# Sums of squares along rows on ScalarE, key stores on ScalarE's queue, and a new order of the preparation steps

## The chip, the cores and the metric

The kernel runs on one core of a Trainium2 chip. The metric is the device time of one execution in microseconds (us). A run of this kernel is timed several times; the runs shown agree within 2.4 us. A profile of one further execution gives the engines' timelines: TensorE (PE in the profile, its weight loads PEld), VectorE (DVE), ScalarE (ACT), GpSimd (POOL) and SyncE (SP), which here only issues DMAs. ScalarE can issue DMAs too, on a queue of its own.

## The reference

One layer over 2048 latent tokens and 256 context tokens of width 1024, all in float32. What matters here is how it begins: each token is normalized, scaled and shifted, and then projected by one wide matrix.

```python
def _rmsnorm(x, g):
    xf = x.astype(jnp.float32)
    xf = xf * lax.rsqrt(jnp.mean(xf * xf, axis=-1, keepdims=True) + EPS)
    return (xf * g.astype(jnp.float32)).astype(x.dtype)
...
        mod = jax.nn.silu(c) @ w_ada[i] + b_ada[i]
        mod_c = jax.nn.silu(c_ctx) @ w_ada[i] + b_ada[i]
        shift, scale, gate = mod[:, None, :D], mod[:, None, D:2 * D], mod[:, None, 2 * D:]
...
        h_lat = _rmsnorm(x, norm_g[i]) * (1.0 + scale) + shift
        h_ctx = _rmsnorm(ctx, norm_g[i]) * (1.0 + scale_c) + shift_c
...
    na_q, na_k, na_v, na_g, r_q, r_k, r_v, r_g = _split_proj(h_lat @ w_in)
    cna_q, cna_k, cna_v, cna_g, cr_q, cr_k, cr_v, cr_g = _split_proj(h_ctx @ w_in)
```

After the projection come a neighbourhood attention, a two-way retention, gates, an output projection, the residual and a last normalization. The change touches none of these.

## The kernel before

Tokens lie along the columns: h is kept as 8 slices of 128 features (k = 0 to 7) by tokens. The host hands the kernel x both as it is (rows of tokens) and transposed. A float32 product is made of three fast ones: each operand is split into a high part (hi) and the rest (lo), and TensorE adds hi by hi, hi by lo and lo by hi. So h has to be ready as hi and lo before TensorE can use it.

**Windows.** The first stage computes the attention keys, in five windows of tokens: windows 0 to 3 take 512 latent tokens each (block 0 to 3), window 4 the 256 context tokens. A window has 32 steps; one step is one feature slice k of one unit, which is three matmuls (`tform`, L357). The four units of a window are four groups of 128 key columns. In window 0 the steps of the four units are mixed in an order written out by hand (`STEPS`, L63), so that slices of h are used as they get ready; its units end at steps 24, 28, 30 and 31. In the other windows the units follow one another, 8 steps each.

**Preparation.** Between the steps the other engines prepare h. The order is written out by hand in `PLAN` (L39): each entry has the step after which it is issued, the action, and its numbers. Each engine works off its own instructions in the order in which they are issued, and so does each DMA queue; an instruction that waits holds up all that follow on its engine. Latent tokens are prepared in pieces of 256 (i = 0 to 7, i = 8 is the context), each in two halves of four slices (u = 0, 1). Piece i belongs to block i // 2. The actions for a piece, in order:

- `x` (`load_x`): load the transposed piece, two DMAs of 512 KB on SP's queue.
- `sq` (`squares`): ScalarE squares it, POOL and VectorE add the eight slices up to one.
- `cs` (`colsum`): TensorE adds over the 128 features of a slice by four tiny matmuls (L209).
- `rs` (`rstd`, `spread_copy`): VectorE scales the sum, POOL raises it to the power -1/2, VectorE copies this r into a tile `t0` of 128 columns per token group.
- `sp` (`spread`): TensorE turns it into a row of r for each token, in every partition (L227).
- `mu` (`spread_mul`): VectorE multiplies x by it (L241), one half at a time.
- `ab` (`prep_ab`): scale and shift, slice by slice, on VectorE (L272) or ScalarE (L274).
- `hl` (`prep_hl`): ScalarE casts to hi (L279), POOL or VectorE subtracts for lo (L283). Eight steps later SP stores the half for later use (`hS`, L253).

Block 0 (i = 0, 1) has `p` (`prep_first`, L255) in place of `ab` and `hl`, one slice at a time. The scale and shift come from the modulation, in four column groups u: `s` splits a weight, `m` multiplies (L311), `ar` (`ada_row`) copies the row out of PSUM, `af` (`ada_fin`) turns it into columns and finishes with `mods` (L332).

**Buffers.** The pool `st` has four tiles of 512 KB; weights of the first units, squares and the context piece go through it in turn. Tiles named `o` have two buffers; both the modulation rows and the evicted keys use them. PSUM has six banks for units, column sums and spreads.

**Evicting the keys** (`u_k`, L380). When a unit ends, ScalarE casts its PSUM bank into `o` (L383), VectorE subtracts for the rest (L384), and the tile is stored to `kS`, 512 KB in windows 0 to 3. `store` (L149) defers the DMA by a number of ticks; a tick comes at the end of each unit, after its eviction. With 1, the store is issued right behind the unit's own eviction. The queue for it is SP's until window 4, and ScalarE's from there on.

After window 4 follow the context units (L809), values, and the other projections.

Of the kernel before, what the change touches and what calls it, by code (L numbers as in the profile page):

```python
# [9 lines left out]
F32 = mybir.dt.float32  # L10
# [3 lines left out]
ALU = mybir.AluOpType  # L14
# [4 lines left out]
P = 128  # L19
# [63 lines left out]
def hybrid_kernel(ctx: ExitStack, tc: tile.TileContext, a: dict, out: bass.AP):  # L83
# [34 lines left out]
    def pool(st, name, bufs, **kw):  # L118
        return st.enter_context(tc.tile_pool(name=name, bufs=bufs, reuse_waits="tile", **kw))
# [11 lines left out]
    env = dict(pp=pool(psx, "pp", 6, space=PSUM), st=pool(sx, "st", 4, side="right"), queue=nc.sync)  # L131

    def ptile(p=None):
        return (p or env["pp"]).tile([P, 512], F32, name="mm")
# [58 lines left out]

    def squares(i):
        sqs[i] = []
        for u in range(2):
            sq = xsq[i][u] if i < 2 else env["st"].tile([P, KH, 256], F32, name="st")
            nc.scalar.activation(sq, raw[i][u], AF.Square)
            eng = (nc.gpsimd, nc.vector)[u]
            eng.tensor_tensor(sq[:, 0:2, :], sq[:, 0:2, :], sq[:, 2:4, :], ALU.add)  # L200
            eng.tensor_tensor(sq[:, 0, :], sq[:, 0, :], sq[:, 1, :], ALU.add)
            sqs[i].append(sq)
        nc.vector.tensor_tensor(sqs[i][0][:, 0, :], sqs[i][0][:, 0, :], sqs[i][1][:, 0, :], ALU.add)

    def colsum(*ii):
        pm = ptile(None if ii[0] < 4 else psm)
        for j, i in enumerate(ii):
            for t in range(2):
                nc.tensor.matmul(pm[:, 2 * j + t:2 * j + t + 1], sqs[i][0][:, 0, t * P:(t + 1) * P], one, start=True, stop=True)  # L209
            rms[i] = pm[:, 2 * j:2 * j + 2]  # L210

    def rstd(i):
        r = env["st"].tile([P, 2], F32, name="rs", bufs=4)
        nc.vector.tensor_scalar(r, rms[i], 1.0 / D, EPS, ALU.mult, ALU.add)
        nc.gpsimd.tensor_tensor(r, r, mhalf[:, 0:2], ALU.pow)
        rbs[i] = r

    def spread_copy(i):
        rbs[i, 1] = env["st"].tile([P, 2, P], F32, name="t0", bufs=2)
        nc.vector.tensor_copy(rbs[i, 1], rbs[i].unsqueeze(2).to_broadcast([P, 2, P]))  # L220
# [95 lines left out]
    def ada_row(u):  # L316
        rows[u] = op.tile([P, 2, 512], F32, name="o")[:, 0, :]
        n = 4 if SPL[u] else 2
        (nc.scalar.copy, nc.vector.tensor_copy)[u % 2](rows[u][0:n, :], aps[u][0:n, :])
# [60 lines left out]
    def u_k(w, c0, ct, b):  # L380
# [4 lines left out]
        store(kS[c0 % 512 // P + ct][:, :, tok], f(o)[:, :, :n])  # L385
# [81 lines left out]
    acts = dict(sq=squares, cs=lambda *i: colsum(*i), rs=lambda i: (rstd(i), spread_copy(i)), sp=lambda *i: spread(*i),  # L467
# [23 lines left out]
    def window(b):  # L491
        units = [u_k(w01, 512 + 256 * g, ct, b) for g in range(2) for ct in range(2)]
        left = [KC] * 4
        for n, u in enumerate(STEPS if b == 0 else [u for u in range(4) for _ in range(KC)]):
            if b == 4 and n == 0:
                env["queue"] = nc.scalar
# [1128 lines left out]
```

## Time and profile before

| | |
|---|---|
| median of 3 runs | 1353.99 us (1352.1 to 1354.42) |
| the profiled execution's own time | 1357.11 us |
| its span, first to last instruction | 1355.2 us |
| TensorE busy | 1310.4 us (97%) |
| VectorE, ScalarE, POOL busy | 834.4, 606.1, 578.2 us |
| window 0 begins, window 4 ends | about 27.5 and 163.9 us |

In the timeline a row has the start, the length, engine, line and operation, what it writes and reads, the shape, the count, and in brackets the idle time of the engine before it with what ended it. A wait for several things is put down to the one that came last in the profile. In the table by stretch, behind the stretch and its length, each engine has its busy time and, in brackets, its instructions, and then come the granted clock of TensorE as a share of full speed, the busy share of the DMA engines, and GB/s. Groups of instructions have the count, then busy time and the mean length in ns, then the idle time before them. DMA rows show the busy share of the DMA engines in tenths over 40 equal slices of the stretch.

### The profile page before, as it was taken

To read this page: it belongs to the slowest core of one execution; us is meant where nothing else is said; L and a number is where in the kernel's file an instruction comes from. 1 tells how busy PE (TensorE), PEld (TensorE's weight loads), DVE (VectorE), ACT (ScalarE), POOL (GpSimd) and SP (SyncE) were. 2 spreads that over 40 slices of the span, in tenths; PEclk is the share of its full clock that TensorE was granted. 3 is DMA by queue.
4 is the path that set the end of the run, shared out by engine and by line. 5 is a ranking of instruction groups with operands and counts; after the bars stand their busy time and mean duration, and the time that the engine had idled before them with its cause. 6 is when DMAs were issued, how large, how long until landed. Compare 5 with 4: busy or idle time off the path is not lost.

```text
span 1355.2 us, 23103 instructions
## 1 busy us (share of the span) xinstructions
PE 1310.4 (97%) x8236; PEld 1148.7 (85%) x8236; DVE 834.4 (62%) x1444; ACT 606.1 (45%) x1259; POOL 578.2 (43%) x569
## 2 busy tenths in 40 slices
PE   6999999999999999999999999999999899999997
PEld 2477999887898888998999889889999789888886
DVE  5686356776666754477767777776655634445345
ACT  4354343333633343555655466556642244333432
POOL 4442101545114664354535465655423154544442
PEclk9999999999999999999999999999999999999999
DMA  9386788565966657977587877776538888445433
GB/s 364 135 279 233 257 286 232 189 204 192 345 161 218 206 180 244 240 222 200 147 226 207 231 217 210 189 189 192 154 100 298 263 294 265 159 165 171 163 121 129
DMA packets 172086, 287.26 MB, mean 212 GB/s; under 512 B 17345, under 2 KB 92225, under 8 KB 170690
## 3 DMA queue, kind: packets, MB, share of 16 engines
q1 hardware_dynamic: 139554, 228.35, 56.1%
q10 hardware_dynamic: 32416, 57.42, 11.7%
q8 instruction: 66, 1.08, 0.3%
q14 instruction: 50, 0.41, 0.1%
HBM read 194.48 MB, written 91.23 MB: 211 GB/s over the span
## 4 chain that ended last, share of the span: by engine, by line
PE 77%; DVE 6%; DMA 6%; POOL 4%; issue 3%; ACT 3%; SPq 1%; ACTq 0%; POOLq 0%; DVEq 0%
PE mm L374 20%; PE mm L671 17%; PE mm L1466 11%; PE mm L363 7%; PE sS L1028 4%; PE tr L1055 3%; PE po L1076 3%; PE mm L1190 2%; PE mm L311 2%; PE tr L1057 2%; PE po L1078 2%; DMA v<-rvS 1%; POOL hlo L531 1%; PE mm L1378 1%; PE mm L1377 1%
## 5 line engine op out<-in xcount | busy, mean ns | idle before, releaser
L374 PE MATMUL mm<-whi,hlo 128*128 128x256 f32 x832 | 228.8, 283 | 1.4 <-DMA hlo<-cS 1.4
L374 PE MATMUL mm<-whi,hhi 128*128 128x256 f32 x768 | 224.5, 292 | 0.0
L374 PE MATMUL mm<-wlo,hhi 128*128 128x256 f32 x768 | 217.2, 283 | 0.0
L1059 ACT CAST pt<-tr 128x640 fp32r<-128x640 f32 (+1 forms) x128 | 95.6, 747 | 160.8 <-PE tr L1057 158.2
L1065 DVE TENSOR_TENSOR pt<-tr,pt 128x640 fp32r<-128x640 f32 (+1 forms) x128 | 113.9, 890 | 78.5 <-ACT pt L1059 77.1
L374 PEld LDWEIGHTS mm<-whi,hlo 128*128 128x128 f32 x832 | 156.7, 191 | 1.8 <-DMA hlo<-cS 1.7
L1048 POOL TENSOR_SCALAR sp<-sp,stt 128x640 f32<-128x640 f32 (+2 forms) x128 | 103.1, 808 | 106.8 <-DVE stt L1047 76.1
L374 PEld LDWEIGHTS mm<-whi,hhi 128*128 128x128 f32 x768 | 146.4, 191 | 0.0
L374 PEld LDWEIGHTS mm<-wlo,hhi 128*128 128x128 f32 x768 | 146.2, 190 | 0.2 <-DVE wlo L347 0.2
L625 POOL TENSOR_TENSOR whi<-st,whi 128x512 fp32r<-128x512 f32 x48 | 64.7, 1369 | 161.1 <-ACT whi L624 160.0
L1037 DVE CUSTOM_DVE_ANT_0 sp<-sS,nb 128x640 f32<-128x640 f32 (+2 forms) x128 | 105.6, 825 | 34.2 <-PE sS L1028 27.8
L1042 ACT ACTIVATE sp<-sp,stt 128x640 f32<-128x640 f32 (+2 forms) x128 | 107.4, 839 | 20.2 <-DVE stt L1037 19.1
L363 PE MATMUL mm<-hhi,whi 128*128 128x512 f32 x256 | 108.5, 424 | 0.0
L363 PE MATMUL mm<-hlo,whi 128*128 128x512 f32 x256 | 102.4, 400 | 6.0 <-DVE hlo L265 2.1
L1028 PE MATMUL sS<-k,q 128*128 128x256 f32 (+3 forms) x512 | 99.2, 316 | 5.4 <-DVE stt L1037 5.1
L363 PE MATMUL mm<-hhi,wlo 128*128 128x512 f32 x256 | 102.4, 400 | 0.3 <-DVE wlo L347 0.3
L1466 PE MATMUL mm<-wor,y 128*128 128x512 f32 x384 | 95.7, 398 | 2.1 <-DVE xt L1475 1.1
L671 PE MATMUL mm<-hhi,whi 128*128 128x512 f32 x336 | 97.4, 394 | 0.0
L1475 DVE TENSOR_TENSOR xt<-mm,xt 128x512 f32<-128x512 f32 x64 | 43.9, 687 | 83.9 <-PE mm L1466 83.9
L1028 PEld LDWEIGHTS sS<-k,q 128*128 128x128 f32 x512 | 82.8, 188 | 12.5 <-DVE stt L1037 8.7
L1466 PE MATMUL mm<-won,y 128*128 128x512 f32 x336 | 90.0, 406 | 0.0
L1466 PEld LDWEIGHTS mm<-wor,y 128*128 128x128 f32 x384 | 69.9, 188 | 18.5 <-issue 3.5
(258 smaller groups left out, 3039.6 us busy)
## 6 DMA issues: line engine op xcount, KB each, us to landing
st<-in_w_in_dram SPq DMA_DIRECT2D x64, 512.0 KB
q<-qS SPq DMA_DIRECT2D x64, 256.0 KB
hlo<-hS SPq DMA_DIRECT2D x20, 512.0 KB
k<-kS SPq DMA_DIRECT2D x16, 576.0 KB
kS<-o SPq DMA_DIRECT2D x16, 512.0 KB
vB<-o SPq DMA_DIRECT2D x64, 128.0 KB
qS<-o ACTq DMA_DIRECT2D x16, 512.0 KB
woS<-g ACTq DMA_DIRECT2D x32, 256.0 KB
```

The costliest lines, as they stand in the source:

```text
L363: nc.tensor.matmul(pm[:, :n], ww[:, k, cs], h[:, k, :], start=(k == 0 and i == 0), stop=(k == KC - 1 and i == 2))
L374: nc.tensor.matmul(pm[:, t * WG:(t + 1) * WG], h[:, k, o:o + P], ww[:, k, :], start=(k == 0 and i == 0), stop=(k == KC - 1 and i == 2))
L625: nc.gpsimd.tensor_tensor(t[:, 1], r, f(t)[:, 0], ALU.subtract)
L671: nc.tensor.matmul(pm, ww[:, k, :], hh[:, k, :], start=(k == 0 and i == 0), stop=(k == KH - 1 and i == 2))
L1028: nc.tensor.matmul(o, hd["q"][i][:, hl, j * P:(j + 1) * P], k, start=(hl == 0), stop=(hl == 1))
L1037: nc.vector.tensor_tensor_reduce(T["sp"][:, :n], T["s"], nbz[big][:, o:o + n], -1.0, 3e38, ALU.add, ALU.min, T["st"][:, 0:1])
L1042: nc.scalar.activation(sp[:, :n], sp[:, :n], AF.Exp, bias=st[:, 0:1], scale=-1.0, accum_out=st[:, 1:2])
L1048: nc.gpsimd.tensor_scalar(sp[:, :n], sp[:, :n], st[:, 2:3], 0.0, ALU.mult, ALU.add)
L1059: nc.scalar.copy(pt[:, :ng_ + 2, 0, :], tr[:, :ng_ + 2, :])
L1065: nc.vector.tensor_tensor(pt[:, :n, 1, :], tr[:, :n, :], f(pt)[:, :n, 0, :], ALU.subtract)
L1466: nc.tensor.matmul(pm, yy[:, k, :], ww[:, k, sl], start=(k == 0 and i == 0), stop=(k == 3 and i == 2))
L1475: nc.vector.tensor_tensor(xts[t][:, sl], pm, xts[t][:, sl], ALU.add)
```

## The change

- Pieces 2 to 8 get their sums of squares from x as rows of tokens. A new action `xt` loads two tiles of 128 tokens by 1024 features (512 KB each, on SP's queue, through `st`). `squares` is then two instructions of ScalarE, each of which also adds up along its row. The adds on POOL and VectorE and the four tiny matmuls of `cs` go for these pieces. Pieces 0 and 1 stay as they were.
- For pieces 2 to 8 the scaling of the sum and the copy into `t0` go from VectorE to POOL, where the power already is.
- The modulation row of group 2 is copied by VectorE, not ScalarE.
- Key stores are on ScalarE's queue from the start, and deferred by two ticks: the store of a unit is issued behind the next unit's eviction.
- `PLAN` is new: slices 7 and 6 of block 0 come at steps 17 and 18, ahead of the scaling of block 1; the `mu` of pieces 2 and 3 (first halves) moves to step 14; block 1's `hl` moves from steps 28 and 29 to 18 to 22; squares of pieces 5 and 6 both come at step 33, their `rs` at 35, spread 5 at step 40 (50 before); block 2's `hl` moves from steps 55 to 61 to 46 to 50. Loads of x and the new row loads are placed anew. From step 68 on the order is that of before, without `sq`, `cs` and `rs`.

```diff
-    (4, 's', 2, 0), (4, 'x', 4), (4, 'p', 2), (5, 'sq', 2), (7, 'm', 2, 0), (8, 'm', 2, 1), (9, 'p', 3),
...
+    (-1, 'p', 1), (-1, 'm', 1, 3), (-1, 'ws', 1), (0, 'ar', 1), (3, 'af', 1), (4, 'xt', 2), (4, 'xt', 3), (4, 'mu', 1, 1),
+    (4, 's', 2, 0), (4, 'x', 4), (4, 'p', 2), (7, 'm', 2, 0), (8, 'm', 2, 1), (9, 'p', 3), (9, 'sq', 2), (9, 'sq', 3),
+    (9, 'm', 2, 2), (9, 'm', 2, 3), (9, 'ar', 2), (10, 'xt', 4), (10, 'x', 5), (11, 'xt', 5), (12, 'mu', 0, 1),
+    (12, 'af', 2), (12, 'm', 3, 0), (12, 'p', 5), (12, 'm', 3, 1), (12, 'p', 4), (12, 'rs', 2), (12, 'rs', 3),
+    (13, 'm', 3, 2), (13, 'm', 3, 3), (13, 'ar', 3), (14, 'sp', 2, 3), (14, 'mu', 2, 0), (14, 'mu', 3, 0), (14, 'sq', 4),
+    (14, 'blk', 1), (15, 'xt', 6), (16, 'af', 3), (17, 'rs', 4), (17, 'p', 7), (18, 'p', 6), (18, 'x', 6),
+    (18, 'ab', 2, 0), (18, 'ab', 3, 0), (18, 'hl', 2, 0), (18, 'hl', 3, 0), (18, 'mu', 2, 1), (18, 'mu', 3, 1),
+    (19, 'ab', 2, 1), (20, 'ab', 3, 1), (21, 'hl', 2, 1), (22, 'hl', 3, 1), (26, 'sp', 4), (28, 'mu', 4, 0),
+    (30, 'mu', 4, 1), (33, 'sq', 5), (33, 'sq', 6), (35, 'rs', 5), (35, 'rs', 6), (36, 'xt', 7), (36, 'ab', 4, 0),
+    (38, 'x', 7), (40, 'sp', 5), (40, 'sq', 7), (41, 'mu', 5, 0), (42, 'rs', 7), (42, 'ab', 4, 1), (42, 'mu', 5, 1),
+    (43, 'ab', 5, 0), (45, 'blk', 2), (45, 'ab', 5, 1), (46, 'hl', 4, 1), (46, 'hl', 4, 0), (46, 'xt', 8),
+    (48, 'hl', 5, 0), (50, 'hl', 5, 1), (50, 'x', 8), (55, 'blk', 3), (60, 'sq', 8), (68, 'sp', 6), (70, 'rs', 8),
...
-    env = dict(pp=pool(psx, "pp", 6, space=PSUM), st=pool(sx, "st", 4, side="right"), queue=nc.sync)
+    env = dict(pp=pool(psx, "pp", 6, space=PSUM), st=pool(sx, "st", 4, side="right"), queue=nc.scalar)
...
+    def load_xt_(i):
+        sqs[i] = []
+        src = a["ctx"] if i == 8 else a["x"][i * 256:(i + 1) * 256, :]
+        for t in range(2):
+            xt = env["st"].tile([P, KH, 256], F32, name="st").rearrange("p k t -> p (k t)")
+            nc.sync.dma_start(xt, src[t * P:(t + 1) * P, :])
+            sqs[i].append(xt)
+
     def squares(i):
+        if i >= 2:
+            rms[i] = env["st"].tile([P, 2], F32, name="rs", bufs=4)
+            for t, xt in enumerate(sqs[i]):
+                nc.scalar.activation(xt, xt, AF.Square, accum_out=rms[i][:, t:t + 1])
+            return
...
     def rstd(i):
-        r = env["st"].tile([P, 2], F32, name="rs", bufs=4)
-        nc.vector.tensor_scalar(r, rms[i], 1.0 / D, EPS, ALU.mult, ALU.add)
+        r = rms[i] if i >= 2 else env["st"].tile([P, 2], F32, name="rs", bufs=4)
+        (nc.gpsimd if i >= 2 else nc.vector).tensor_scalar(r, rms[i], 1.0 / D, EPS, ALU.mult, ALU.add)
...
-        nc.vector.tensor_copy(rbs[i, 1], rbs[i].unsqueeze(2).to_broadcast([P, 2, P]))
+        (nc.gpsimd if i >= 2 else nc.vector).tensor_copy(rbs[i, 1], rbs[i].unsqueeze(2).to_broadcast([P, 2, P]))
...
-        (nc.scalar.copy, nc.vector.tensor_copy)[u % 2](rows[u][0:n, :], aps[u][0:n, :])
+        (nc.scalar.copy, nc.vector.tensor_copy)[u > 0](rows[u][0:n, :], aps[u][0:n, :])
...
-        store(kS[c0 % 512 // P + ct][:, :, tok], f(o)[:, :, :n])
+        store(kS[c0 % 512 // P + ct][:, :, tok], f(o)[:, :, :n], 2)
...
-            if b == 4 and n == 0:
-                env["queue"] = nc.scalar
```

More of the change, by code (lines that the diff above doesn't have):

```diff
@@ L192, in hybrid_kernel @@
     sqs, rms, rbs, prs = {}, {}, {}, {}
-    def squares(i):
+    def load_xt_(i):
[5 more added lines that the diff above has]
+            sqs[i].append(xt)
+    def squares(i):
+        if i >= 2:
[3 more added lines that the diff above has]
+            return
         sqs[i] = []
         for u in range(2):
-            sq = xsq[i][u] if i < 2 else env["st"].tile([P, KH, 256], F32, name="st")
+            sq = xsq[i][u]
             nc.scalar.activation(sq, raw[i][u], AF.Square)
@@ L205, in colsum @@
     def colsum(*ii):
-        pm = ptile(None if ii[0] < 4 else psm)
+        pm = ptile()
         for j, i in enumerate(ii):
@@ L466, in hybrid_kernel @@
         lds[name](*args)
-    acts = dict(sq=squares, cs=lambda *i: colsum(*i), rs=lambda i: (rstd(i), spread_copy(i)), sp=lambda *i: spread(*i),
+    acts = dict(sq=squares, xt=load_xt_, cs=lambda *i: colsum(*i), rs=lambda i: (rstd(i), spread_copy(i)), sp=lambda *i: spread(*i),
                 mu=lambda i, u: spread_mul(i, (u,)), ab=prep_ab, hl=prep_hl, blk=alloc_blk, x=load_x, w=lambda: wr.append(w_raw(2560)),
```

21 rows, old and new, of the table PLAN are left out of this document.

## The prediction

> **What bounds the kernel now.** I read the page first, then the busy times by stretch, then the timeline of TensorE, and last the other engines where TensorE waits.
>
> ```profile
> span 1355.2 us, 23103 instructions
> PE 1310.4 (97%) x8236; PEld 1148.7 (85%) x8236; DVE 834.4 (62%) x1444; ACT 606.1 (45%) x1259; POOL 578.2 (43%) x569
> ...
> sum 230.00, PE 210.21 PEld 162.29 DVE 142.36 ACT 100.56 POOL 66.00; mean PE 9.14 PEld 7.06 DVE 6.19 ACT 4.37 POOL 2.87
> ...
> 38.00:42.00 4.00, 4.00 (x6) 0.56 (x6) 3.84 (x7) 0.00 (x0) 0.82 (x1) 0.58 1.04 411
> 76.00:79.50 3.50, 3.45 (x9) 2.72 (x10) 3.50 (x3) 2.59 (x4) 3.50 (x2) 0.53 0.97 229
> ```
>
> TensorE is busy for all but 45 us, and 20 of these lie in the first 230 us, where the change works. Ten of the 20 are the first loads, which stay. The two short stretches are busy too, but at a granted clock (third number from the end) of 0.58 and 0.53. The rest is the waits in the TensorE timeline (in brackets: idle before, and releaser):
>
> ```profile
> 37.92 0.50 PE L363 MATMUL mm<-hlo,whi 128*128 128x512 f32 x1 [1.70 <-DVE hlo L265]
> 66.77 0.47 PE L363 MATMUL mm<-hlo,whi 128*128 128x512 f32 x1 [0.37 <-DVE hlo L265]
> 76.05 0.63 PE L363 MATMUL mm<-hlo,whi 128*128 128x512 f32 x1 [1.96 <-DVE hlo L283]
> 79.46 0.47 PE L363 MATMUL mm<-hhi,whi 128*128 128x512 f32 x1
> 84.98 0.50 PE L209 MATMUL mm<-one,st 128*128 128x1 f32 x4
> 85.35 0.47 PE L363 MATMUL mm<-hhi,whi 128*128 128x512 f32 x1
> 102.52 0.50 PE L363 MATMUL mm<-hlo,whi 128*128 128x512 f32 x1 [1.44 <-POOL hlo L283]
> 107.95 0.71 PE L227 MATMUL mm<-ident,t 128*128 128x128 f32 x4 [1.51 <-DVE t L220]
> 110.24 0.58 PE L209 MATMUL mm<-one,st 128*128 128x1 f32 x4 [0.17 <-DVE st L203]
> 171.60 0.39 PE L374 MATMUL mm<-wlo,chi 128*128 128x256 f32 x1 [0.76 <-DVE wlo L347]
> ```
>
> These are waits for prepared h: the last pieces of block 0, block 1 at the start of window 1 (76.05), block 2 at the start of window 2 (102.52). VectorE and POOL end them. The two longest are followed by a slow stretch: from 76.05 to 79.46 nine matmuls take about 1.6 us more than nine at the later pace.
>
> **The change part by part.** *Column sums out.* Seven groups of four L209 matmuls go (blocks 2 to 8 of 256 tokens). One group holds the next matmul up by 85.35 - 84.98 = 0.37 us, so 7 x 0.37 = 2.6 us: 1.1 before step 40 of the plan, 1.5 after.
>
> *Adds out, row loads in.*
>
> ```profile
> L200 POOL TENSOR_TENSOR st<-st 128x512 f32<-128x512 f32 x7 | 10.4, 1487 | 13.0 <-ACT st L198 13.0
> L200 DVE TENSOR_TENSOR st<-st 128x512 f32<-128x512 f32 x7 | 5.9, 842 | 0.7 <-ACT st L198 0.7
> L198 ACT ACTIVATE st<-hlo 128x1024 f32<-128x1024 f32 x4 | 4.0, 1044 | 0.0
> L1422 ACT ACTIVATION_READ_ACCUMULATOR ot<-xt x32: 185/187/224, 1160.6 to 1349.5; 128x1 f32 x32
> ...
> 33.80 0.40 DVE L263 TENSOR_SCALAR hhi<-hhi,mods 128x256 f32<-128x256 f32 x1
> 35.57 1.36 DVE L263 TENSOR_SCALAR hhi<-hhi,mods 128x256 f32<-128x256 f32 x1
> 69.68 0.70 POOL L215 TENSOR_TENSOR rs<-rs,mhalf 128x2 f32<-128x2 f32 x1 [3.34 <-DVE rs L214]
> L1383 POOL TENSOR_SCALAR rss<-rss x16: 192/193/198, 1111.8 to 1306.5; 128x4 f32<-128x4 f32 x16
> L220 DVE COPY t<-rs x9: 294/294/1350, 19.1 to 127.5; 128x256 f32<-128x256 f32 x9
> ```
>
> VectorE loses 5.9 us in L200 alone and further, shorter adds; POOL loses 10.4. ScalarE's squares stay two of 1.04 us per block, plus an accumulator read of 0.19 (from a like form). A POOL copy to 128x256 isn't in the trace: not under VectorE's 0.29, not over the 1.49 of the 512-column two-input add; I take 0.5, nearest the one-input row. So r costs POOL 0.19 + 0.70 + 0.5 = 1.4 us per block. The 1.36 us of the L263 at 35.57 is 0.96 over the same form at 33.80, and a removed POOL add ran beside it. I take 1.1 us off the 1.70 wait, and with it the slow stretch after (0.58 of the clock for 4 us: 1.7 us). Seven MB of row loads come on SP's queue:
>
> ```profile
> DMA  0000000000000000000000000000000000000000
> GB/s 25 6 0 0 0 0 0 0 0 0 13 0 0 0 0 0 0 0 0 0 0 0 0 0 0 0 0 0 0 0 0 0 0 0 0 0 0 0 0 0
> ```
>
> This is 46 to 72 us; at the 411 GB/s of the 38 us row 7 MB are 17 us. Five of the seven fit into that hole, and nothing is late: blocks 2 and 3 land near 45.5, before their scale is there. Without the hole they would stand ahead of the transposed loads, 2.5 us each.
>
> *Block 0's last pieces and block 1 sooner.* With 1.1 + 1.7 + 0.7 (two L209 groups) saved by then, the modulation is ready near 58.4 instead of 61.4, and the 0.37 wait goes. From there ScalarE and VectorE alternate:
>
> ```profile
> 61.40 0.16 DVE L332 SCALAR_TENSOR_TENSOR mods<-mods,ng 128x4 f32<-128x4 f32 x1
> 61.60 2.08 ACT L262 ACTIVATE hhi<-hhi,mods 128x256 fp32r<-128x256 f32 x4 [7.86 <-DVE mods L332]
> L241 DVE TENSOR_TENSOR hlo<-hlo,mm 128x1024 f32<-128x1024 f32 x4 | 4.8, 1212 | 0.5 <-PE mm L227 0.5
> L274 ACT ACTIVATE hlo<-hlo,mods 128x256 f32<-128x256 f32 x8 | 4.3, 595 | 1.4 <-DVE hlo L241 1.4
> L279 ACT CAST hhi<-hlo 128x1024 fp32r<-128x1024 f32 x4 | 4.1, 1041 | 0.6 <-DVE hlo L272 0.6
> L283 POOL TENSOR_TENSOR hlo<-hlo,hhi 128x1024 fp32r<-128x1024 f32 x2 | 5.2, 2616 | 2.5 <-ACT hhi L279 2.5
> L283 DVE TENSOR_TENSOR hlo<-hhi 128x1024 fp32r<-128x1024 f32 x2 | 2.4, 1218 | 0.6 <-ACT hhi L279 0.6
> ```
>
> ScalarE: p7 and p6 to 60.6, four L274 and two L279 to 64.9. VectorE: L283 to 66.1, two L241 to 68.5. ScalarE: two L274 to 69.6, two L279 to 71.7; POOL's L283 for the second half of 2 ends near 73.3, VectorE's near 72.9. TensorE starts window 1 near 69 and wants that half at step 36, near 71.4: a wait of 1.9 in place of 1.96 + 1.6. Up to step 40: 1.1 + 1.7 + 1.1 + 0.4 + 3.6 - 1.9 = 6.0 us gained; TensorE ends step 40 near 77.6 instead of 83.6 (27 matmuls into window 1: the tenth starts at 79.46, then 0.23 each, as 24 of them fill the time to 84.98).
>
> *Key stores.* Here is the price. Eviction tiles o have two buffers, so eviction n+2 waits until store n has landed, and store n is now issued on ScalarE's queue behind eviction n+1.
>
> ```profile
> 76.53 0.54 SPq L151 DMA_DIRECT2D kS<-o  x1
> 82.82 0.59 ACT L383 CAST o<-mm 128x512 fp32r<-128x512 f32 x1 [4.23 <-DVE st L203]
> 126.03 5.61 SPq L151 DMA_DIRECT2D kS<-o  x2
> DMA  9999999999999999999999999973000000000000
> 156.43 0.60 ACTq L151 DMA_DIRECT2D kS<-o  x1
> 166.33 0.37 ACT L383 CAST o<-mm 128x256 fp32r<-128x256 f32 x1 [4.50 <-DMA kS<-o]
> ```
>
> The eviction at 82.82 needed the buffer of the store issued at 76.53 (VectorE's own use of it was long over): 6.3 us under load. Alone, a store takes 2.8: issued at 126.03, all DMA quiet from 128.8 (fourth row: 126 to 130 in 40 slices). The worst is 9.9, 156.43 to 166.33. In window 0 the four units end at steps 24, 28, 30 and 31, so the chain is bare. Evictions 1 and 2 stand behind the last cast of block 1 (71.7): done near 72.9. VectorE's half of the first (0.69) follows its L283: store 1 at 73.5, landed 76.3 (SP stands at a row load that waits for squares 5, so nothing else is under way). Eviction 3 to 76.9, store 2, landed 79.7; eviction 4 to 80.3, store 3 issued by 80.85. Only then squares 5: 83.2; r on POOL: 84.7. TensorE has spread 5 at step 40 and stands from 77.6 to 84.7: 7.1 us, and 1.7 of slow clock after, since waits of 1.70 and 1.96 brought one. Bounds: 0, if ScalarE gets there 7 us sooner, and 7.1 + 2 x 3.5 = 14.1, if two landings take 6.3. I take 7.1 + 1.7 = 8.8; the queue is idle, so the 2.8 row is the near one. What waits behind ScalarE there (squares 6, block 4's bias, the next eviction) has until step 64 and ends near 100 for TensorE's 103.
>
> In windows 1 to 3 a unit lasts 5.5 us against 2.8 plus an eviction: covered. In window 4 units last 2.9 us and the chain is bare again, but before has one too, which ends in the 0.76 wait at 171.60: I take 0, with -1.3 and +5 as ends.
>
> *Later.* Block 2's half sooner, r without L203 and L214: the waits of 1.44, 1.51 and 0.17 go, and four L209 groups (1.5): 4.6 us.
>
> **Sum.** -6.0 + 8.8 - 4.6 = -1.8 us. The profiled span 1355.2 becomes 1353.4; that execution took 1357.11 with 1.9 around it, so 1355.3. It ran 3.1 over the median of the runs, 1353.99; against the median the forecast is 1352.2 us.
>
> Two rules of the Trainium skill bear on this, and the sum stands without them. "TensorE: Matmul & The Clock Gate", Part 1, has the clock halved only after an idle window of about 3.4 us; the trace has it after 1.70 and 1.96. By the rule these slow stretches need not go with their waits; that is the last rival below. "DMA: Bandwidth & Descriptors", queues, rings and completion order, has each DMA engine alternate between the queues' rows, so ScalarE's store would not stand behind SP's loads; the 9.9 us of 156.43 speak against it. By the rule window 4 would give its -1.3: 1350.9.
>
> **The rivals.** *The chain misses TensorE* (chance 0.25): if block 1's casts end 5 us sooner, near 67, the wait at step 40 is 2.1 with no slow clock: -6.0 + 2.1 - 4.6 = -8.5, 1345.5 us. For it: VectorE and POOL lose much work there; against: the alternation has no slack in the rows above. *Window 4 stalls* (0.20, slower): the loads of block 1's h and of weights stand in the DMA queue, one landing takes 9.9 instead of 6, and the weight casts of the context units come behind it on ScalarE. It decides once they end later than TensorE's end of window 4, 11.4 us after its start; 4.6 late, plus 1.7 slow clock, less the 1.3 already there: +5.0, 1357.2. For it: the 9.9 row; against: SP is free earlier and its loads too. *The h isn't sooner* (0.07): the plan puts block 2 at steps 46 to 50, but ScalarE, held by stores, reaches it when it did before; the 1.44 wait stays and so do the others: near 1354. *The slow stretches stay* (0.08): the clock falls at 38 and 76 us whatever the waits do, and the 1.7 and 1.6 aren't gained: 1.5 us slower, 1355.5. For it: the waits of 1.44 and 1.51 brought no slow matmuls, so a wait alone isn't the whole cause; against: both stretches begin right at a wait. By the first rule of the skill above this is what happens.
>
> **How the numbers follow.** The forecast has 0.40, with its own range 1349 to 1355. A measurement of this kernel tells about 0.2% (2.7 us) from no change. Faster by more: 0.25, and 0.16 of the forecast's; slower: 0.20, and 0.04 of the last two rivals and the forecast's edge; within: 0.35. The range from 1344.5 to 1358 takes in the first rival and the window 4 price and leaves out two in ten, mostly a longer chain.
>
> **What would show it.** Right: a single long TensorE wait near 77 for L227, released by POOL's t, with ScalarE's L383 waiting for kS twice before it; no wait for block 2. Wrong: no such wait (first rival), or a wait over 3 us after window 4 before L374 (second), or squares 5 standing ahead of eviction 4 on ScalarE. If the slow clock near 38 us stays, 1.7 us of the sum falls.

## The result, and the profile after

The changed kernel takes 1361.39 us (median of six runs, 1359.41 to 1365.78), the kernel before 1353.92 beside it (1352.03 to 1355.9): 1.0066 times as long, 95% interval 1.005 to 1.0082. (This ratio is estimated from the runs and is not the quotient of the two medians, which is 1.0055.) It is slower, by 7.5 us, and lies above the range. The profiled executions differ less, 1359.6 against 1355.2 us of span, since the one of before ran some 3 us over its median; what the two traces show of the loss is these 4.4 us.

The page of the changed kernel, its first lines:

```profile
span 1359.6 us, 23049 instructions
PE 1307.7 (96%) x8208; PEld 1147.9 (84%) x8208; DVE 814.6 (60%) x1410; ACT 607.7 (45%) x1272; POOL 566.5 (42%) x569
```

VectorE has lost 19.8 us and POOL 11.7, as meant, and TensorE stands longer: 51.9 us not busy, where it was 44.8. Its timeline gives the places (in brackets the idle time before, and the releaser):

```profile
70.76 0.47 PE L376 MATMUL mm<-hhi,whi 128*128 128x512 f32 x1 [1.00 <-DVE hlo L254]
76.36 0.47 PE L376 MATMUL mm<-hlo,whi 128*128 128x512 f32 x1 [2.17 <-DVE hlo L296]
87.59 1.22 PE L240 MATMUL mm<-ident,t 128*128 128x128 f32 x4 [6.20 <-POOL t L233]
129.81 0.50 PE L376 MATMUL mm<-hlo,whi 128*128 128x512 f32 x1 [0.70 <-DVE hlo L296]
168.65 0.39 PE L387 MATMUL mm<-whi,chi 128*128 128x256 f32 x1 [4.49 <-ACT whi L358]
169.91 0.58 PE L387 MATMUL mm<-wlo,chi 128*128 128x256 f32 x1 [0.76 <-DVE wlo L360]
```

(L376 is the window matmul, L363 before; L387 the matmul of the units after window 4, L374 before; L240 the spread, L227 before; L254 the multiplication by r, L241 before; L292 the cast to hi and L296 the lo subtraction, L279 and L283 before; L396 and L397 the eviction, L383 and L384 before; L358 and L360 the cast and subtraction that split a weight, L345 and L347 before; L527 the read of block 1's h out of `hS`, L516 before.) Two of these matmuls in the timeline of the kernel before, the second of window 3 and the first of the context units:

```profile
129.82 0.40 PE L363 MATMUL mm<-hlo,whi 128*128 128x512 f32 x1
163.91 0.28 PE L374 MATMUL mm<-whi,chi 128*128 128x256 f32 x1
```

At the start of window 3 the kernels are level, 129.81 and 129.82. At the first context unit the changed one is 4.7 us late, and at the next long pause of before (171.60, now 177.23) 5.6. From there the distance stays at 5 to 6 us for most of the program, and 4.3 are left at the last matmul. Window 4's own matmuls are not late (the last one starts at 163.88, and at 163.79 before). So the time went at the end of window 4, in front of the context units; what came before it cancelled out.

The busy times by stretch (the third number from the end is the granted clock) show the slow clock behind the three long waits:

```profile
70.00:76.00 6.00, 3.43 (x13) 2.36 (x13) 4.24 (x6) 4.55 (x8) 2.37 (x1) 1.00 0.01 5
76.00:82.00 6.00, 5.04 (x14) 3.70 (x14) 4.36 (x6) 0.59 (x1) 0.00 (x0) 0.72 0.37 136
87.00:90.50 3.50, 2.91 (x9) 2.52 (x10) 0.92 (x2) 3.50 (x8) 1.77 (x5) 0.50 0.93 284
170.00:176.00 6.00, 6.00 (x40) 6.00 (x41) 1.80 (x4) 1.51 (x3) 0.00 (x0) 0.77 0.77 246
```

And ScalarE's timeline with its queue (ACTq) shows the two chains of stores, in windows 0 and 1 and in window 4:

```profile
73.54 1.05 ACT L396 CAST o<-mm 128x512 fp32r<-128x512 f32 x2
76.85 0.58 ACTq L151 DMA_DIRECT2D kS<-o  x1
80.00 0.59 ACT L396 CAST o<-mm 128x512 fp32r<-128x512 f32 x1 [5.41 <-DMA kS<-o]
83.19 0.59 ACT L396 CAST o<-mm 128x512 fp32r<-128x512 f32 x1 [2.60 <-DMA kS<-o]
83.83 1.06 ACT L206 ACTIVATE st<-st 128x1024 f32<-128x1024 f32 x1
...
152.81 0.52 ACTq L151 DMA_DIRECT2D kS<-o  x1
163.49 0.37 ACT L396 CAST o<-mm 128x256 fp32r<-128x256 f32 x1 [10.10 <-DMA kS<-o]
166.68 0.37 ACT L396 CAST o<-mm 128x256 fp32r<-128x256 f32 x1 [2.82 <-DMA kS<-o]
167.55 1.99 ACT L358 CAST whi<-st 128x1024 fp32r<-128x1024 f32 x2 [0.50 <-DVE o L397]
```

The store issued at 152.81, behind the fourth eviction of window 3, is that of the window's third unit; the first eviction of window 4 needs its buffer and waits 10.1 us for it. A second wait of 2.82 follows, and then come the weight casts L358 for which TensorE stands until 168.65. SP's queue at that time:

```profile
128.24 23.45 SPq L176 DMA_DIRECT2D st<-in_w_in_dram  x4
151.78 2.17 SPq L527 DMA_DIRECT2D hhi<-hS  x4
```

The last of four weight loads (151.35) and three of the four reads of block 1's h (512 KB each) were issued in the 1.5 us before the store, the fourth read just behind it. In the kernel before the order was another (SP's queue, then ScalarE):

```profile
154.06 0.53 SPq L151 DMA_DIRECT2D kS<-o  x1
154.68 2.43 SPq L516 DMA_DIRECT2D hhi<-hS  x4
...
159.84 2.00 ACT L345 CAST whi<-st 128x1024 fp32r<-128x1024 f32 x2 [1.05 <-DVE o L384]
```

There all stores of window 3 were out ahead of the reads, and the first two evictions of window 4 (155.57 and 158.42) waited for no store. The late one, issued at 156.43, held up the third eviction only, and the weight casts stood ahead of that.

The DMA view by queue shows how the store of 152.81 spends its time (packets, MB, share of the DMA engines; q1 is SP's queue, q10 ScalarE's, which alone moves data from 164 to 166, when only the next store is under way). First 153 to 157.9 us, then 158 to 163.2:

```profile
q1 hardware_dynamic: 325, 1.20, 96.0%
```

```profile
q1 hardware_dynamic: 356, 1.26, 60.6%
q10 hardware_dynamic: 271, 0.52, 25.9%
```

Until 157.95, 5.1 us after its issue, nothing of the store moves, while SP's queue does; then the two queues move side by side for another 5 us.

### The profile page after: what moved, and what is told of

It is laid out like the page before. It is cut to its first block, busy times and chain, and to the rows that moved or that the text cites. A ratio compares the mean times of both kernels' runs of the same rounds, so it can differ in the third digit from the quotient of the medians.

```text
span 1359.6 us, 23049 instructions
## 1 busy us (share of the span) xinstructions
PE 1307.7 (96%) x8208; PEld 1147.9 (84%) x8208; DVE 814.6 (60%) x1410; ACT 607.7 (45%) x1272; POOL 566.5 (42%) x569
## 4 chain that ended last, share of the span: by engine, by line
PE 71%; DMA 6%; DVE 4%; POOL 4%; ACT 3%; issue 2%; ACTq 0%; SPq 0%; POOLq 0%; DVEq 0%
PE mm L387 20%; PE mm L682 17%; PE mm L1477 11%; PE sS L1039 4%; PE mm L376 4%; PE tr L1066 3%; PE po L1087 3%; PE mm L1201 2%; DMA kS<-o 2%; PE tr L1068 2%; PE po L1089 1%; DMA v<-rvS 1%; POOL hlo L542 1%; PE mm L1389 1%; PE mm L1388 1%
## 5 line engine op out<-in xcount | busy, mean ns | idle before, releaser
L387 PE MATMUL mm<-whi,hlo 128*128 128x256 f32 x832 | 228.5, 282 | 1.0 <-DMA hlo<-cS 1.0
L387 PE MATMUL mm<-whi,hhi 128*128 128x256 f32 x768 | 224.2, 292 | 0.0
L387 PE MATMUL mm<-wlo,hhi 128*128 128x256 f32 x768 | 216.9, 282 | 0.4 <-DVE wlo L360 0.4
L387 PEld LDWEIGHTS mm<-whi,hlo 128*128 128x128 f32 x832 | 156.5, 191 | 1.4 <-DMA hlo<-cS 1.3
L387 PEld LDWEIGHTS mm<-wlo,hhi 128*128 128x128 f32 x768 | 146.1, 190 | 0.6 <-DVE wlo L360 0.6
L387 PEld LDWEIGHTS mm<-whi,hhi 128*128 128x128 f32 x768 | 146.3, 190 | 0.0
L376 PE MATMUL mm<-hhi,whi 128*128 128x512 f32 x256 | 108.7, 425 | 1.0 <-DVE hlo L254 1.0
L376 PE MATMUL mm<-hlo,whi 128*128 128x512 f32 x256 | 102.4, 400 | 4.0 <-DVE hlo L296 2.9
L376 PE MATMUL mm<-hhi,wlo 128*128 128x512 f32 x256 | 102.4, 400 | 0.3 <-DVE wlo L360 0.3
```

What stands on the lines that cost most here:

```text
L376: nc.tensor.matmul(pm[:, :n], ww[:, k, cs], h[:, k, :], start=(k == 0 and i == 0), stop=(k == KC - 1 and i == 2))
L387: nc.tensor.matmul(pm[:, t * WG:(t + 1) * WG], h[:, k, o:o + P], ww[:, k, :], start=(k == 0 and i == 0), stop=(k == KC - 1 and i == 2))
```

## The experiments

The ratios are to the kernel before, timed beside each kernel on the same chip. Where an expectation speaks of block 4 to 8 in squares, r, rows or casts, it means the piece of that number.

**What makes window 4 late.** Three kernels take one side each. x2 moves the reads of block 1's h out of the way:

```diff
-            if b == 4 and n % 8 == 0:
-                raw_piece(0, n // 8)
+            if b == 3 and n in (12, 16, 20, 24):
+                raw_piece(0, n // 4 - 3)
```

> The changed kernel with the four loads of block 1's h (2 MB, hS into hhi) issued at steps 12 to 24 of window 3 in place of steps 0 to 24 of window 4. Load theory (the first key store of window 4 lands after 10 us because these loads stand before it in the DMA engines): it lands within 5 us, the waits of 4.5 and 0.8 us after window 4 go, 5 to 6 us less than the changed kernel, 1355 to 1357 us; spread 5 still waits 6 us. Rival (the chain of four stores is too long whatever stands in the queue, or ScalarE's queue is served late): the landing stays near 10 us and the time near 1361.

1357.22 us, 1.0024 (1.0012 to 1.0037): 4.2 below the changed kernel. ScalarE's timeline in window 4:

```profile
155.39 0.52 ACTq L151 DMA_DIRECT2D kS<-o  x1
159.31 0.37 ACT L396 CAST o<-mm 128x256 fp32r<-128x256 f32 x1 [3.41 <-PE mm L376]
```

This is the same store, and the first eviction of window 4 now waits for its own unit on TensorE and not for it: at most 3.9 us from issue to eviction, where it was 10.7. In the DMA view the store's 0.52 MB move from 1.2 us behind the issue and are through by 158.3. TensorE has no wait left at the context units; a new one of 2.04 us, for POOL's lo of the context, stands at the start of window 4.

x3 leaves the reads and puts the key stores back as before (SP's queue, right behind their own eviction, ScalarE's queue from window 4 on):

```diff
-    env = dict(..., queue=nc.scalar)
+    env = dict(..., queue=nc.sync)
...
-        store(kS[...], f(o)[:, :, :n], 2)
+        store(kS[...], f(o)[:, :, :n])
...
+            if b == 4 and n == 0:
+                env["queue"] = nc.scalar
```

> The changed kernel with the key stores as before: SP's queue until window 4, issued right behind their own eviction. Store-chain theory: after window 4 only the 1.3 us of waits of the kernel before are left, 4 to 5 us less; at spread 5 little is gained, since evictions 3 and 4 still wait for stores 1 and 2 and the stores now stand among the spills on SP's queue: a wait of 5 to 9 us; 1355 to 1358 us in all. Rival (it is only the queue and the later issue that cost, in window 0 too): both waits go, 1349 to 1352 us.

1356.54 us, 1.0028 (1.0016 to 1.004), as expected. The waits at the context units shrink to 0.40 and 0.76:

```profile
172.75 0.39 PE L387 MATMUL mm<-whi,chi 128*128 128x256 f32 x1 [0.40 <-ACT whi L358]
174.01 0.39 PE L387 MATMUL mm<-wlo,chi 128*128 128x256 f32 x1 [0.76 <-DVE wlo L360]
```

The wait at spread 5 stays, 8.8 us: on SP's queue, between copies of h, the stores there land no sooner, and ScalarE's two waits for kS are 5.57 and 5.22.

x5 is the converse: the kernel before, with the stores alone moved.

```diff
-    env = dict(..., queue=nc.sync)
+    env = dict(..., queue=nc.scalar)
...
-        store(kS[...], f(o)[:, :, :n])
+        store(kS[...], f(o)[:, :, :n], 2)
...
-            if b == 4 and n == 0:
-                env["queue"] = nc.scalar
```

> The kernel before, with only the key stores moved: on ScalarE's queue from the start, one unit later. Theory (the loss is window 4, where a store on ScalarE's queue lands late behind the loads of block 1's h and of weights, and the moved stores make it so): a wait of 3 to 6 us after window 4 before L374, and 1357 to 1360 us. Rival (the stores alone are harmless, and window 4 stalls only because the whole schedule stands otherwise by then): window 4 waits as in the kernel before (0.8 to 1.5), 1352 to 1355 us.

1364.83 us, 1.0087 (1.0062 to 1.0113), more than was expected. ScalarE in window 4, and then TensorE at window 2 and at the context units:

```profile
167.03 0.37 ACT L383 CAST o<-mm 128x256 fp32r<-128x256 f32 x1 [10.46 <-DMA kS<-o]
```

```profile
104.53 0.80 PE L363 MATMUL mm<-hlo,whi 128*128 128x512 f32 x1 [2.83 <-POOL hlo L283]
171.90 0.43 PE L374 MATMUL mm<-whi,chi 128*128 128x256 f32 x1 [4.57 <-ACT whi L345]
```

The same 10.5 and 4.6 us without any other part of the change, so the moved stores are enough. They also make block 2 later (2.83 at window 2 where before has 1.44), and of the 8.0 us by which this trace is late at the first context unit 3.3 are there at the start of window 4 already. By the two ratios the rest of the change would gain about 0.002 of the time, 3 us, but the intervals overlap, so this isn't shown. x3 and x5 move the queue and the later issue together; which of the two it takes, no run tells.

x6 gives the kernel before the sooner reads of x2 and nothing else (the same edit).

> The kernel before, with only the four reads of block 1's h issued in window 3 (steps 12, 16, 20, 24) and not in window 4. Theory (these reads stand ahead of the stores of window 4 in both kernels): the 0.76 wait after window 4 goes, and 1352.5 to 1353.5 us, 0.4 to 1.3 us sooner than before. Rival (they matter only beside the moved stores): 1353.5 to 1354.5.

1352.38 us, 0.9992 (0.9979 to 1.0006): 0.95 below the kernel before beside it, the size that was expected, but not to be told from no change. The 0.76 wait shrank to 0.5.

**Whether spread 5 can be had sooner.** x1 takes squares and r of pieces 5 and 6 ahead of the evictions:

```diff
-    ... (33, 'sq', 5), (33, 'sq', 6), (35, 'rs', 5), (35, 'rs', 6), ...
+    ... (23, 'sq', 5), (23, 'sq', 6), (23, 'rs', 5), (23, 'rs', 6), ...
```

> The changed kernel with the squares and r of pieces 5 and 6 moved from steps 33 and 35 to step 23, ahead of the first key eviction on ScalarE; nothing else. Store-chain theory (spread 5 stands because squares 5 stand behind two store landings): TensorE's wait of 6.2 us at L240 and the slow clock after it go, 5 to 8 us less than the changed kernel, 1353 to 1356 us; the waits of 4.5 and 0.8 us after window 4 stay. Rival (the seven MB of row loads or the accumulating squares are what costs): the wait moves but the time stays near 1361.

1366.84 us, 1.0097 (1.0075 to 1.0119), above both expectations. The wait at spread 5 is gone, so squares 5 behind the landings did make it, and window 2 begins with two others. TensorE, and ScalarE ahead of it:

```profile
104.89 0.79 PE L376 MATMUL mm<-hhi,whi 128*128 128x512 f32 x1 [8.52 <-ACT hhi L292]
109.54 0.79 PE L376 MATMUL mm<-hlo,whi 128*128 128x512 f32 x1 [3.86 <-POOL hlo L296]
```

```profile
77.94 0.58 ACTq L151 DMA_DIRECT2D kS<-o  x1
85.98 0.59 ACT L396 CAST o<-mm 128x512 fp32r<-128x512 f32 x1 [8.31 <-DMA kS<-o]
```

The squares set buffers free, the loads of piece 7 start on SP's queue just then, and the first store lands 8 us after its issue. x4 adds the edit of x2 to this one.

> Both edits: squares and r of pieces 5 and 6 at step 23, loads of block 1's h in window 3. If the two waits are separate and both causes are right, the gains add up: 10 to 14 us less than the changed kernel, 1348 to 1351 us, faster than the kernel before by 0.2 to 0.4%. Rival (the second stall grows when the first one goes, since TensorE then reaches the stores sooner): 1353 to 1357 us.

1361.78 us, 1.0064 (1.0044 to 1.0084), above both expectations again: no wait is left at the context units, and it is 5 us below x1, but window 2 waits 8.2 and 3.9 as in x1. x8 is x1 with the stores put back as in x3.

> The changed kernel, with the squares and r of blocks 5 and 6 at step 23, ahead of the evictions, and the key stores issued as in the kernel before. Theory (what holds ScalarE in window 0 and 1 is the landing of the stores, and with the squares early they land late only because on ScalarE's queue they go behind the row and transposed loads that the squares set free; on SP's queue they are issued ahead of those): ScalarE is through with the fourth eviction near 86, not 97; no wait at spread 5, a wait of 0 to 4 us at the start of window 2, window 4 as before; 1349 to 1354 us. Rival (a store takes 5 us or more on either queue there, and the wait only moves): a wait over 6 us at the start of window 2, 1355 to 1359 us.

1362.34 us, 1.0067 (1.0046 to 1.0088), above both ranges. The wait at window 2 is 9.28 us, as the rival has it, but not for its reason: ScalarE has the third and fourth eviction at 81.92 and 87.84, near what the theory had, and then stands for something else:

```profile
98.42 1.06 ACT L206 ACTIVATE st<-st 128x1024 f32<-128x1024 f32 x1 [7.38 <-DMA st<-in_x_dram]
```

Squares 7 (step 40) stand ahead of piece 5's casts and wait for rows that are still coming. x11 moves them, and their r, to steps 52 and 54.

> The kernel of x8 (squares and r of blocks 5 and 6 at step 23, key stores as before) with squares 7 and their r moved from steps 40 and 42 to 52 and 54, behind the h of block 5. Theory (in x1 and x8 ScalarE stands 7.4 us for the rows of block 7, in front of block 5's casts, and this makes the wait of 9.3 at the start of window 2): that wait falls to 0 to 3 us, and since window 2 then begins 6 to 9 us sooner and window 4 stalls little there, 1350 to 1357 us. Rival (the casts are late anyway, because of the stores or of POOL): a wait over 5 us, 1358 to 1362 us.

1362.84 us, 1.0082 (1.0055 to 1.0108): a miss. The wait of 9.3 at the start of window 2 falls to 1.6, as the theory had it, but a second one of 4.1 stays there, and window 3 now begins with 7.2. x12 takes all causes away at once: squares 5 at step 23, squares 6 and 7 at 52, the edits of x2 and x3, and that of x10 below. x13 is x12 with the stores as the changed kernel has them.

> The changed kernel with squares and r of block 5 at step 23, those of blocks 6 and 7 at 52 and 54, the key stores as before, the four reads of block 1's h in window 3, and the lo parts of block 1 on VectorE alone: every cause found so far taken away at once. Theory (the causes are separate, and the sooner h is worth what it was meant to be): no wait over 3 us between window 0 and window 4, 1345 to 1350 us, faster than both kernels. Rival (TensorE is then held by the next thing, the landing of the stores in windows 0 and 1): waits of 5 us or more in all, 1351 to 1355 us.

> The same as x12, but with the key stores on ScalarE's queue one unit later, as the changed kernel has them. Theory (the store on ScalarE's queue is what costs, wherever loads stand on SP's queue): 4 to 10 us slower than x12, most of it in window 0 to 2 where ScalarE waits for kS, since the reads of block 1's h no longer stand ahead in window 4. Rival (the queue matters only in window 4, and there the sooner reads have taken care of it): within 2 us of x12.

1360.74 (1.0061, 1.0044 to 1.0079) and 1358.11 us (1.0053, 1.003 to 1.0075): x12 is above both its ranges, and between the two queues no difference is to be told, as the rival of x13 has it. In x12 the waits for ScalarE's and POOL's part of h (us in total, times, longest) add up to what was won:

```profile
PE mm L376 <- ACT hhi L292: 8.0, 2, 7.2
PE mm L376 <- POOL hlo L296: 4.2, 1, 4.2
```

TensorE reaches window 2 at 94 us, 11 us sooner than in the changed kernel, stands 4.2 there and 7.2 at window 3, and enters window 3 at 131.6, 2.9 later than the changed kernel. In x16 the cast of block 3 waits for a copy of h going out (row below); in x12 the trace puts the end of this cast's wait down to TensorE, and what held it there stays open.

**VectorE's lo beside POOL's.** In the changed kernel the second half of block 1's lo took VectorE 2.55 us and not 1.22. The group of L296 by engine (count: shortest, median, longest in ns), changed kernel, then x10, in which VectorE does both halves:

```profile
L296 POOL TENSOR_TENSOR hlo<-hlo,hhi x2: 2372/2386/2400, 64.9 to 72.8; 128x1024 fp32r<-128x1024 f32 x2
L296 DVE TENSOR_TENSOR hlo<-hlo,hhi x2: 2546/2562/2577, 65.8 to 73.7; 128x1024 fp32r<-128x1024 f32 x2
```

```profile
L296 DVE TENSOR_TENSOR hlo<-hlo,hhi x4: 1218/1223/1227, 64.1 to 71.9; 128x1024 fp32r<-128x1024 f32 x4
```

```diff
-LOV = {0: 2, 1: 2, 2: 0, 3: 3, ...
+LOV = {0: 2, 1: 2, 2: 3, 3: 3, ...
```

> The changed kernel, with the lo parts (L296) of both halves of block 1 on VectorE, where POOL had one of the two. Theory (VectorE's L296 takes 2.55 us because POOL's runs beside it and holds it up until it has ended): four L296 of 1.22 us on VectorE, the last one ending near 74 and not 76.2; the 2.2 us wait of window 1 falls below 0.7, its slow stretch (0.72) goes or shrinks; the wait at spread 5 grows by about what is won there less 1 us; 1358.5 to 1360.5 us. Rival (the 2.55 has another cause, such as loads landing at the same time): four of about 2.5, the last one ending after 78, the wait grows by 2 us or more, 1362 to 1364 us.

1358.77 us, 1.0044 (1.0024 to 1.0064), 2.6 below the changed kernel. Four subtractions on one engine take less time than two on each, and the last ends at 73.1 instead of 76.2; the wait at window 1 falls from 2.17 to 0.95, with no slow clock behind it, and spread 5 waits 7.9. x14 makes this edit in x6.

> The kernel of x6 (before, with the four reads of block 1's h in window 3) with both lo parts of the first half of block 1 on VectorE, where POOL had one. Theory (VectorE's L283 of 2.8 us there stood behind POOL's as in the changed kernel): the 2.0 wait in window 1 falls below 1 and its slow stretch shrinks; 1349.5 to 1352 us, 1 to 2.5 below x6. Rival (there the two did not meet, since before's wait comes from VectorE's own adds): within 1 us of x6, 1351.5 to 1353.5.

1353.79 us, 1.0007 (0.9989 to 1.0025): nothing that can be told. The wait at window 1 fell only to 1.48, and that at window 2 rose from 1.56 to 2.45.

**The parts apart.** x15 is the kernel before with the row-wise sums alone: the squares, row loads and r of the change, no column sums from piece 2 on, and also the VectorE copy of the modulation row of group 2; stores and the rest of the plan as before. Its plan against that of before:

```diff
-... (5, 'sq', 2), ...
+... (4, 'xt', 2), (4, 'xt', 3), ... (9, 'sq', 2), ... (10, 'xt', 4), ...
+... (20, 'xt', 5), ... (28, 'xt', 6), ... (53, 'xt', 7), ... (79, 'xt', 8), ...
-... (13, 'cs', 2, 3), ... (23, 'cs', 4), ... (42, 'cs', 5), ... (62, 'cs', 6), ... (70, 'cs', 7), ... (90, 'cs', 8), ...
```

> The kernel before with one part of the change alone: squares by rows on ScalarE with their row loads, r on POOL, no column sums from block 2 on; the other steps of the plan, the order of block 0's last pieces and the key stores as before. Theory (the gains of the forecast that come from the sums themselves are real: 2.6 us of L209, 1.1 of the first wait with 1.7 of slow clock, 1.5 of the wait for t): 1347 to 1351 us, faster than before. Rival (TensorE's time in windows 0 to 4 is set by the h of each block, whose ScalarE, loads and stores the sums do not shorten, so that the waits only come back elsewhere): 1352 to 1356 us.

1351.63 us, 0.9991 (0.9976 to 1.0007): the direction of the theory and a size that can't be told from nothing. Traced against the kernel before, TensorE is 6.0 us ahead at the end of window 1, waits 2.85 for block 2, and is 5.3 ahead at the end of window 4; between the two spans 2.8 are left. Both of these executions ran over the medians of their runs, by 2.6 and 3.1 us. x16 adds the edits of x2 and x10 to x15, and x17 is the changed kernel with the edits of x2, x3 and x10.

> x15 with the four reads of block 1's h in window 3 and with the lo parts of block 1's first half on VectorE alone. Theory: 1 to 3 us below x15, 1345 to 1349 us, faster than both kernels by more than the measurement is uncertain. Rival (nothing before the loop over the weights is worth more than 2 us, since a later block's h makes good what an earlier one won): within 1.5 us of x15 and of before.

> The changed kernel with the key stores as before, the four reads of block 1's h in window 3 and the lo parts of block 1 on VectorE alone; squares 5 stay at step 33. Theory (the three edits took 4.9, 4.2 and 2.6 us off alone, the first two for the same wait): 1352 to 1355 us, no wait over 1.5 us at window 4, a wait of 7 to 9 us at spread 5 as before the edits. Rival (the stall moves on to windows 2 and 3 as in x12): 1356 to 1360.

x16: 1349.73 us, 0.9979 (0.9968 to 0.999), faster than both kernels, by a little, and 0.7 above the range that was expected. x17: 1355.47 us, 1.0028 (1.0018 to 1.0037), just above its range, with 0.76 us the longest wait behind window 4, 1.84 at window 2 and 9.1 us at spread 5. So with the same mending the sooner plan is about 6 us slower than the old one. TensorE in x17, and in x16 ahead of windows 1 and 2, with ScalarE's first cast of block 3 in x16:

```profile
85.92 1.22 PE L240 MATMUL mm<-ident,t 128*128 128x128 f32 x4 [9.14 <-POOL t L233]
```

```profile
69.93 0.50 PE L376 MATMUL mm<-hlo,whi 128*128 128x512 f32 x1 [0.76 <-DVE hlo L296]
96.89 0.79 PE L376 MATMUL mm<-hlo,whi 128*128 128x512 f32 x1 [3.52 <-POOL hlo L296]
```

```profile
111.43 1.05 ACT L292 CAST hhi<-chi 128x1024 fp32r<-128x1024 f32 x1 [2.35 <-DMA hS<-hhi]
```

In x16 TensorE is at window 1 six us sooner than in the kernel before, and waits 3.52 at window 2 where that waited 1.44. Block 3's hi lies in a tile that held block 2's h before its split, so the cast has to wait until that copy has landed in `hS`. A third buffer for `o` would test the chain of stores directly; no run has one.

## Why the prediction was wrong

The forecast was -1.8 us, and what came is the stall that its second rival describes, behind window 4, with a larger loss than the rival's. Step by step:

*Column sums out and the first wait.* Forecast 1.1 + 1.7 for the wait near 38 us and its slow clock. TensorE is 2.6 us ahead there and 4.0 by step 29 of window 0. Right in these two executions. But of the four kernels that still have this wait only two show the slow clock behind it (before and x5, not x6 and x14; last section), so the 1.7 is a gain over this execution of the kernel before, and may be none over its median.

*Gain to step 40.* Forecast 6.0, measured 2.5. TensorE is 6.5 ahead of the kernel before at the point where that one had left its own wait in window 1, and then loses 2.17 in its wait for L296 (forecast 1.9, near it) and 1.6 in the slow clock after it, which the sum left out although it allows for one at the next wait. The wait of 0.37 in window 0, which was to go, is there with 0.52, and a wait of 1.00 at the start of window 1, for L254, was not foreseen. The term behind the 1.00 and the 2.17 is VectorE's L296 at 1.22 us: it takes 2.55 while POOL's half runs, and L254 stands behind the first of the two. x10 shows that this is the cause: there the wait of 1.00 is gone and the longer one falls to 0.95. The 1.22 came from the row of the form with one buffer name (hlo<-hhi). Block 1 has the other form, and the group of L283 by form in the kernel before had it, once short and once long:

```profile
L283 DVE TENSOR_TENSOR hlo<-hlo,hhi x2: 1210/2008/2807, 74.7 to 76.4; 128x1024 fp32r<-128x1024 f32 x2
```

*The chain of stores before spread 5.* The mechanism, its place and its sign were right: two waits for kS, squares 5 behind them, one long wait for spread 5 released by POOL's t. Forecast 7.1 + 1.7; measured 6.20 and about 2.2 (2.45 ahead before, 6.0 behind after). The chain itself ran 2.9 us late, 87.6 and not 84.7: block 1's last cast ended at 73.6 and not 71.7, and the second part of the first eviction stood behind the second long L296, which ended at 76.2 and not 72.9, so store 1 went out at 76.85 and not 73.5. The stores landed in about 3 us as taken, r on POOL took 0.19 + 0.70 + 0.40.

*Later.* Forecast -4.6; from 6.0 behind to level in window 2, -6.0. Right, a little small.

*Window 4.* **This is the step that failed**: "I take 0, with -1.3 and +5 as ends". It cost 5.6. The text held the price (4.6 late, slow clock, +5.0) and the row of 9.9 us, and gave the rival 0.20 because the kernel before lives with the same 9.9. What it didn't follow is which store is late, and on which side of the weight casts its landing is waited for. Before, the stores of window 3 went out on SP's queue ahead of the reads, each right behind its own eviction, and the 9.9 fell on the first store of window 4, which holds up only the third eviction, behind the casts. Now the store of window 3's third unit goes out on ScalarE's queue one unit later and meets the reads: the landing of 10.1 is waited for by the first eviction, 2.82 follows it, and only then come the weight casts, for which TensorE stands 4.5 us. The argument against, that SP is free sooner, was no argument: at 151.78 SP begins to issue the reads, one microsecond ahead of the store. x2, x3 and x5 show this from three sides. The forecast weighed the rule of the Trainium skill's "DMA: Bandwidth & Descriptors" (queues, rings and completion order) by which each DMA engine alternates between the queues' rows and this store would not stand behind SP's loads. The trace bears out half of it: from 158 us on the two queues move side by side, but for the 5.1 us before that nothing of the store moves, against 1.2 us in x2. The waits of 10.1, 10.46 and, in x1, 8.31 have both parts in them; what holds up the start is not shown.

*The sum.* With the sizes measured, -2.5 + 8.5 - 6.0 is level at window 3, and window 4 makes it +5.6, of which 4.4 are left between the two spans. With the rival's +5.0 the text's sum would have been +3.2; the other 2.4 of the 5.6 are the 3.5 us that were not gained by step 40, less 1.1 by which the other terms came out better. The profiled execution of before stood 3.1 us over its median, and the one of the changed kernel at its own; so the loss between the medians is 7.5 us. The text took gains that it had read off that one execution from the median of before.

*The rivals.* The first did not come: the chain held TensorE for 6.2 us. Nor did the third: no wait for block 2 is left at the start of window 2. The fourth, a slow clock that comes whatever the waits do, is half true: the stretch at 38 us went, and another came at 77 (last section).

## What to carry to other kernels

A store on another engine's queue is not out of the way of the loads: where its buffer gates the next eviction, list what the load queue issues in the few microseconds before each such store, stage by stage, and take the late landing for that stage and not the mean. A stage that already lives with one late landing is no proof that it can live with the same landing two evictions sooner in the chain. And work that starts sooner in front of a chain of buffers gains what the chain lets through: here up to 11 us won ahead of window 2 were given back by window 3.

## What the runs showed of the hardware

**A VectorE subtraction with both inputs in SBUF stands while POOL's runs.** 2.55 us beside POOL's 2.39, 1.22 alone; POOL's own time hardly changes (2.40 at 118.8 us, with none of VectorE's beside it). Splitting the pair over both engines took longer than leaving both on VectorE. The Trainium skill's "SBUF — State Buffer" (who interferes with whom) has the rule (the port pair that the two share is an exclusive lock, and the second to come stands until the first is through); the trace agrees, with starts 0.9 us apart, VectorE's second, and ends 1.1 apart, near the 1.22 of one subtraction.

**The same wait brings the slow clock in one execution and not in another.** Kernel before and x6 stand for L265 in window 0 at the same place, 1.70 and 1.71 us. The busy times of the stretches behind it (the third number from the end is the clock), kernel before, then x6:

```profile
38.00:40.00 2.00, 2.00 (x4) 0.43 (x5) 1.88 (x5) 0.00 (x0) 0.15 (x1) 0.66 1.02 408
40.00:42.00 2.00, 2.00 (x3) 0.13 (x1) 1.97 (x3) 0.00 (x0) 0.67 (x1) 0.50 1.05 414
```

```profile
38.00:40.00 2.00, 2.00 (x6) 0.26 (x4) 1.84 (x6) 0.00 (x0) 0.53 (x1) 1.00 1.01 404
40.00:42.00 2.00, 2.00 (x7) 0.75 (x7) 1.71 (x2) 0.00 (x0) 0.30 (x1) 1.00 1.05 414
```

One loses 1.7 us by this and the other nothing. Of the other two kernels with this wait x5 (1.76 us) has the slow stretch and x14 (1.70) has not. Waits of 1.44 and 1.51 brought no slow clock in before's trace, 1.80 none in x15 and 2.04 none in x2; those of 2.17, 6.20 and 4.49 in the changed kernel each did. "TensorE: Matmul & The Clock Gate" of the Trainium skill, Part 1, lets the gate watch windows that run freely, so that the same kernel meets them at another phase each time; that would explain it, but no trace shows the phase. Its 3.4 us of idleness does not agree: half of it was enough at times. A sum that books 1.7 us of slow clock for a wait under 2 us books something that comes by chance.
